# A ring of eight weight tiles, late modulation bound in order, one load per scan system, and gates and attention outputs that stay on chip, in a hybrid attention and DeltaNet block

## The chip, the cores and the metric

The kernel runs on one core of a Trainium2 chip. The metric is the device time of one execution in microseconds; the time before is the median of three runs. The engines are named as in the profile: PE is TensorE (PEld its weight loads), DVE is VectorE, ACT is ScalarE, POOL is GpSimd, and SP is SyncE, which issues most of the DMA transfers. A second queue of DMA issues is ACT's own.

## The reference

One layer over 256 latent tokens and 256 context tokens of width 2048, all in float32. Cut to what matters (heads 8, head width 128, chunk 64):

```python
sh1, sc1, g1, sh2, sc2, g2 = split(silu(c) @ w_ada + b_ada, 6)       # modulation; the context has its own
(lq_a, lkv_a, lk_r, ldq, ldk, ldv, ldz, lda, ldb, lga, lgb) = split_columns(
    modulate(rmsnorm(x, norm_mix), sh1, sc1) @ w_in)                  # and the same for ctx
y_mla = attend_latent(q_l, k_l, v_l, k_c, v_c)       # latent queries over latent and context keys, one softmax

# gated DeltaNet, two directions, chunks of 64: a unit lower triangular system per chunk and head
sol = triangular_solve(m + I, [v * beta, kb * exp(gc)])
v_new = u - w @ s;  s_next = s * g_end + k_end.T @ v_new;  o = (q * exp(gc)) @ s + a @ v_new

y = (sigmoid(lga) * (y_mla @ w_o_mla) + sigmoid(lgb) * (y_dn @ w_o_dn)) @ w_out
x = x + g1 * y
x = x + g2 * conv_glu(modulate(rmsnorm(x, norm_ffn), sh2, sc2), w_ffn_up, ffn_conv, w_ffn_down)
```

The context runs through its own scan first, and its final states start the latent scans. Eight steps of the scan follow each other: four chunks of the context, four of the latent tokens, both directions and all heads side by side.

## The kernel before, in words

**Weights.** Nearly all weights come from DRAM as tiles of 128 x 1024 float32 (512 KB). `raw_w` takes such a tile, named `raw`, from a ring of `NR` buffers (tag "raw", pool `wr`) and issues its load on SP (L127). `split` then makes two parts of it for TensorE: ACT casts the high part `whi` (L121), and DVE subtracts to get the low part `wlo` (L122). TensorE multiplies activations with both. Every matmul is issued through a small wrapper class `Ordered` (L57 to 72) and stands in the profile under its line L68. Where an engine's wrapper is `pinned`, an instruction keeps its place behind the one written before it on that engine; what is not pinned is put in order by a scheduler, from the program's dependences and its own estimates. TensorE is pinned from the attention part on.

**Late modulation.** `ada_rest` computes the part of `w_ada` that is needed late: 128 dots, each one DVE instruction (L279) over a weight tile `rawa` from the same ring (L260) against `sch`. It is a generator that the attention part and the scan advance by a budget (`side`, `fill`), and it loads one tile ahead of its dot.

**Stages, by the time in the profile.** 0 to 56 us: norms, modulation and the first projections (`fp`, `amp`), whose loads are `xl`, `xc`, `wt`, `raw<-in_wadab`, `gr`. Until about 440 us: projections of the DeltaNet inputs (heads, convolution, the key products `U`, `A`). From 440 to 715 us: attention in four passes `b` of two heads each (`mla_project`, `mla_attend`), interleaved with gate projections (`gtp`) and with the inverses of the triangular systems on the side (`inverse`, `off_diagonal`). 715 to 925 us: the DeltaNet scan (`scan`, steps with `kp`, `yp`, `sp`), interleaved with the wd gates' projections and with the attention output's projection (`brp`, weights `womla`). Then the merge, the output projection, and from about 1070 us the ConvGLU.

**Through DRAM.** Results that wait for a later stage lie in DRAM buffers. A triangular system of 64 x 64 is handled as 32 x 32 blocks. `inverse` computes the diagonal blocks in `ux`, a transposed copy is `xt`, and 12 stores on SP (L842) write them to `Xq`; `off_diagonal` computes for q = 0 to 7 the block between them (`uo`) and ACT's queue stores it to `Xo` (L881). In the scan, `load_system` (L1248) collects each step's systems into one of two SBUF tiles `tt` by six DMAs of 32 KB, of which each run in DRAM is 128 bytes; the blocks above the diagonal of a `tt` are zero because POOL cleared the tile once. The gates' `tanh` results `zx` are stored to `Gs` by ACT's queue (L897) and come back as `gt`, four at a time (L1207). Each pass of the attention stores two heads of its output `ryx` to `Ys` (L1140); after the last, the whole of it comes back as `yraw` (1 MB, L1198) and is split into `YM`.

**Queues.** SP and ACT issue their DMAs in program order. Each DMA issue takes one of eight completion semaphores (DMAHW0 to DMAHW7 in the rows below) in turn, for both queues together, and an issue whose semaphore is still held by an earlier DMA waits until that one has landed; the scheduler writes this as a wait.

Of the kernel before, what the change touches and what calls it, by code (L numbers as in the profile page):

```python
# [16 lines left out]
P = 128  # L17
# [12 lines left out]
NR = 5  # L30
# [23 lines left out]
def hybrid_block(ctx: ExitStack, tc: tile.TileContext, io, dbg=None):  # L54
# [45 lines left out]
    dve.memset(ones, 1.0)  # L100
    onesr = const.tile([P, P], F32R, name="onesr")
# [152 lines left out]
    def ada_rest():  # L254
# [9 lines left out]
        half, ahead = None, load(0)  # L264
        for i in range(128):
            c, n = divmod(i, 32)
            h, j = (n // 16 + c) % 2, n % 16
            if h != half:

                for _ in range(1 if i else 0):  # L270
                    yield 1300
                half, sch = h, ad.tile([P, GR], F32, tag="sch", name="sch")
                sync.dma_start(sch, Sc[h])
                for _ in range(3):
                    yield 1300
            w = ahead
            if i < 127:
                ahead = load(i + 1)
            dve.tensor_tensor_reduce(out=w, in0=w, in1=sch, scale=1.0, scalar=0.0, op0=ALU.mult, op1=ALU.add, accum_out=parts[:, h, j : j + 1])  # L279
# [371 lines left out]
    Xq = dram.tile([3, 32, 4, 32, 32], F32, name="Xq")  # L651
    Xo = dram.tile([32, 4, 32, 32], F32, name="Xo")
# [134 lines left out]
    ada.done = 0  # L787
# [30 lines left out]
    def inverse():  # L818
# [20 lines left out]
        for g in range(4):  # L839
            gs = slice(32 * g, 32 * g + 32)  # L840
            for n, x in enumerate((xt, X[:, 0], X[:, 1])):
                sync.dma_start(Xq[n, :, g], x[gs])  # L842
        yield 1000
        pI.close()

    def off_diagonal():
# [7 lines left out]
        def load(q):  # L854
# [4 lines left out]
            for n in range(2):  # L859
                sync.dma_start(xd[:, n], Xq[2 * n, rs].rearrange("r g j c -> (g j) r c"))  # L860
# [4 lines left out]
        for q in range(8):  # L865
# [15 lines left out]
            act.dma_start(Xo[4 * q : 4 * q + 4].rearrange("r g c i -> (g c) r i"), uo)  # L881
# [8 lines left out]
    def gate_fin(ps, out, fin):  # L890
        x = pz.tile([P, T], F32, tag="zx", name="zx")
# [5 lines left out]
        act.dma_start(out, x)  # L897
# [205 lines left out]
    def mla_attend(b):  # L1103
# [29 lines left out]
        def values(h2):  # L1133
# [6 lines left out]
            sync.dma_start(Ys[:, 2 * b + h2], yx)  # L1140
# [30 lines left out]
    tail = iter(())  # L1171
    for b in range(4):
        at, pr = mla_attend(b), mla_project(b + 1) if b < 3 else iter(())
        for n in range(7):
            for st in (pr, tail, at):
                c = next(st, None)
                if c is not None:
                    side(c, R1 if b < 3 else 2.0)
        tail = at
# [5 lines left out]
    gates = gate_tiles([("wgd", f, Gs[1, :, f], None) for f in range(KD)])  # L1185
# [10 lines left out]
    YM = hp.tile([P, HEADS, 2, T], F32R, tag="x16", name="YM")  # L1196
    yraw = pd.tile([P, HEADS, T], F32, tag="o", name="yraw")
    sync.dma_start(yraw, Ys)  # L1198
    split(yraw, YM[:, :, 0], YM[:, :, 1])
# [3 lines left out]
    def branch(w, wh, f, ymat, out):  # L1203

        if f % 4 == 0:
            gt = pd2.tile([P, 4, T], F32, tag="gt", name="gt")
            sync.dma_start(gt, Gs[wh, :, f : f + 4])  # L1207
            gts[wh] = gt
        W = load_w(io[w][f])
# [8 lines left out]
        dve.scalar_tensor_tensor(out=out, in0=gts[wh][:, f % 4], scalar=1.0, in1=ox, op0=ALU.add, op1=ALU.mult)  # L1218
# [5 lines left out]
    def scan():  # L1224
# [5 lines left out]
        for n in range(2):  # L1230
            pool.memset(TTv[n], 0.0)
# [10 lines left out]
        def load_system(n):  # L1242
            st, tt = steps[n], TTv[n % 2]
            for d in range(2):
                for r, c, x in ((0, 0, Xq[1]), (32, 32, Xq[2]), (0, 32, Xo)):
                    rs, cs = slice(64 * d + r, 64 * d + r + 32), slice(c, c + 32)
                    n = 16 * d + 2 * st
                    sync.dma_start(tt[rs, :, cs], x[n : n + 2].rearrange("a g c i -> c (a g) i"))  # L1248
# [122 lines left out]
    fill = Side(e_fill())  # L1371
    pe.pinned = True
# [236 lines left out]
```

## Time and profile before

| | |
|---|---|
| median of 3 runs | 1796.3 us (1796.25 to 1796.43) |
| the profiled execution | 1796.66 us, its span 1794.8 us |
| TensorE busy | 1740.9 us, 97% |
| DVE, ACT, POOL busy | 1353.9, 944.5, 42.1 us |
| DMA | 419.79 MB, 234 GB/s over the span |

The span is what the trace covers, and the execution's own time is 1.9 us longer. Below, a stretch's row gives busy time of each engine, then the clock that TensorE was granted (1.00 is full), the share of time in which the 16 DMA engines were busy (a little over 1 is possible where packets overlap) and the GB/s moved. A row of waits gives total, times and the longest. A row of the timeline gives start, duration, engine, line, operation, and in brackets the idle time before it with what ended it.

### The profile page before, as it was taken

Reading aid. Unit: us, or ns where it says so; the run is one execution under the profiler, and the core shown is the slowest. Engines: PE = TensorE matmul, PEld = TensorE weight load, DVE = VectorE, ACT = ScalarE, POOL = GpSimd, SP = SyncE. Lnnn points to the kernel's source line nnn. Section 1 sums busy time; section 2 is a strip of 40 time slices with the busy share of each in tenths; the row PEclk is TensorE's granted clock in tenths of the full one; section 3 lists DMA queues with packets and bytes.
Section 4 is the critical chain, followed back from the end, with each engine's and each line's share of the span. In section 5 each row is a group of like instructions: output and inputs, shape, how many; then the busy total and the mean of one; then the engine's idle time right before and its main releaser. Section 6 shows DMA issues by size and latency. Waiting matters only on the chain.

```text
span 1794.8 us, 34114 instructions
## 1 busy us (share of the span) xinstructions
PE 1740.9 (97%) x12957; PEld 1504.6 (84%) x12957; DVE 1353.9 (75%) x2692; ACT 944.5 (53%) x1962; POOL 42.1 (2%) x49
## 2 busy tenths in 40 slices
PE   7999999999999999899999989999999999999999
PEld 6787888887888888687878878888888888888888
DVE  4687899879677777576789889887788888755554
ACT  3334544444567666564655546555555555544443
POOL 0000010000000000000010000000000000000000
PEclk9999999999899999999999989999999999999999
DMA  9982788773778767888957966777677777666663
GB/s 383 399 319 89 207 241 241 228 213 104 220 241 260 229 213 249 279 308 309 317 166 240 327 234 224 244 229 229 190 224 226 225 225 225 184 199 199 198 199 122
DMA packets 191493, 419.79 MB, mean 234 GB/s; under 512 B 57248, under 2 KB 97312, under 8 KB 188896
## 3 DMA queue, kind: packets, MB, share of 16 engines
q1 hardware_dynamic: 164144, 402.38, 69.0%
q10 hardware_dynamic: 27184, 15.23, 2.8%
q8 instruction: 102, 1.67, 0.4%
q14 instruction: 63, 0.52, 0.1%
HBM read 388.57 MB, written 28.84 MB: 233 GB/s over the span
## 4 chain that ended last, share of the span: by engine, by line
PE 70%; issue 10%; DMA 9%; DVE 6%; ACT 3%; POOL 1%; SPq 0%; POOLq 0%; DVEq 0%; ACTq 0%
PE fps L68 25%; PE dps L68 13%; PE mmp L68 9%; PE gtp L68 7%; PE fp L68 4%; DMA rawa<-in_wada 4%; DVE wlo L122 2%; PE brp L68 2%; DMA raw<-in_wadab 1%; PE amp L68 1%; DVE rawa L279 1%; DMA raw<-in_wgd 1%; ACT whi L121 1%; PE op L68 1%; DMA raw<-in_wz 1%
## 5 line engine op out<-in xcount | busy, mean ns | idle before, releaser
L122 DVE TENSOR_TENSOR wlo<-raw,whi 128x512 fp32r<-128x512 f32 (+1 forms) x940 | 632.6, 685 | 220.4 <-ACT whi L121 212.1
L121 ACT CAST whi<-raw 128x512 fp32r<-128x512 f32 (+1 forms) x940 | 574.3, 619 | 425.2 <-PE dps L68 113.7
L68 PE MATMUL fps<-H,whi 128*128 128x512 f32 x1376 | 475.1, 394 | 1.7 <-DVE H L1446 1.7
L68 PE MATMUL fps<-H,wlo 128*128 128x256 f32 x1376 | 372.3, 281 | 0.3 <-DVE wlo L122 0.3
L68 PEld LDWEIGHTS fps<-H,whi 128*128 128x128 f32 x1376 | 253.7, 189 | 53.3 <-issue 2.0
L68 PEld LDWEIGHTS fps<-H,wlo 128*128 128x128 f32 x1376 | 259.8, 189 | 7.8 <-DVE wlo L122 0.7
L68 PE MATMUL gtp<-h,whi 128*128 128x512 f32 x640 | 235.1, 404 | 7.4 <-ACT whi L121 7.1
L68 PE MATMUL mmp<-h,whi 128*128 128x512 f32 x640 | 227.1, 397 | 0.0
L68 PE MATMUL dps<-GB,whi 128*128 128x512 f32 (+1 forms) x595 | 195.7, 378 | 0.0
L279 DVE CUSTOM_DVE_ANT_0 rawa<-rawa,sch 128x1024 f32<-128x1024 f32 x128 | 155.8, 1220 | 45.5 <-DMA rawa<-in_wada 41.9
L68 PE MATMUL gtp<-h,wlo 128*128 128x256 f32 x640 | 176.0, 285 | 4.4 <-DVE wlo L122 4.2
L68 PE MATMUL mmp<-h,wlo 128*128 128x256 f32 x640 | 176.0, 281 | 0.6 <-DVE wlo L122 0.6
L68 PE MATMUL dps<-GB,wlo 128*128 128x256 f32 x560 | 154.1, 280 | 0.0
L68 PEld LDWEIGHTS gtp<-h,whi 128*128 128x128 f32 x640 | 121.8, 192 | 34.1 <-ACT whi L121 9.5
L68 PEld LDWEIGHTS mmp<-h,whi 128*128 128x128 f32 x640 | 119.0, 188 | 24.7 <-issue 0.4
L68 PEld LDWEIGHTS gtp<-h,wlo 128*128 128x128 f32 x640 | 122.9, 192 | 11.9 <-DVE wlo L122 7.5
L68 PEld LDWEIGHTS dps<-GB,whi 128*128 128x128 f32 x595 | 109.2, 188 | 21.1
L68 PEld LDWEIGHTS mmp<-h,wlo 128*128 128x128 f32 x640 | 120.3, 188 | 3.9 <-DVE wlo L122 1.3
L68 PEld LDWEIGHTS dps<-GB,wlo 128*128 128x128 f32 x560 | 105.1, 188 | 0.6
L68 PE MATMUL fp<-h,gh 128*128 128x256 f32 (+1 forms) x448 | 85.1, 290 | 2.5 <-ACT h L68 1.7
L68 PEld LDWEIGHTS fp<-h,gh 128*128 128x128 f32 (+1 forms) x448 | 69.4, 189 | 7.6 <-issue 4.1
L517 ACT COPY fx<-fps 128x256 f32<-128x256 f32 x86 | 31.8, 372 | 65.4 <-PE fps L68 65.3
(566 smaller groups left out, 2525.4 us busy)
## 6 DMA issues: line engine op xcount, KB each, us to landing
rawa<-in_wada SPq DMA_DIRECT2D x128, 512.0 KB, 4.7
raw<-in_wgate SPq DMA_DIRECT2D x82, 512.0 KB, 4.3
raw<-in_wval SPq DMA_DIRECT2D x82, 512.0 KB, 4.6
raw<-in_wdown SPq DMA_DIRECT2D x80, 512.0 KB, 4.3
wt<-in_wadas SPq DMA_DIRECT2D x16, 1024.0 KB, 10.8
raw<-in_wadab SPq DMA_DIRECT2D x32, 512.0 KB, 9.2
raw<-in_wgm SPq DMA_DIRECT2D x32, 512.0 KB, 4.7
raw<-in_wgd SPq DMA_DIRECT2D x32, 512.0 KB, 6.1
```

Of the source, the lines that this page charges most:

```text
L68: i = f(*a, **k)
L121: act.copy(hi, raw)
L122: dve.tensor_tensor(out=lo, in0=raw, in1=hi, op=ALU.subtract)
L279: dve.tensor_tensor_reduce(out=w, in0=w, in1=sch, scale=1.0, scalar=0.0, op0=ALU.mult, op1=ALU.add, accum_out=parts[:, h, j : j + 1])
L517: act.copy(out, ps[:M, T:])
```

## The change

- The ring `NR` grows from five tiles to eight. `ada_rest` loads two tiles ahead of its dots, and until the scan begins its dots are issued in order (`odve`), each held behind the DVE instruction written before it; such a dot then shows under the wrapper's line L68.
- A DRAM buffer `Tt` has the layout that the scan reads, zeros included. `inverse` writes the diagonal blocks there by 16 DMAs of 64 KB, `off_diagonal` writes each `uo` by four DMAs of 16 KB on SP, and two DMAs on ACT's queue write the zero blocks from a cleared tile `none`. `load_system` is one DMA of 256 KB. `Xq` keeps only the two parts that `off_diagonal` reads.
- The wd gates from the third on (f = 2 to 15) stay in an SBUF tile `gk`; the other gates go through `Gs` as before.
- `YM` is allocated when the last attention pass begins. Six heads are read back into its low half and split in place, two at a time, during that pass (`heads_back`); the last two heads are split straight from `ryx` and never stored.
- The program reserves 1024 for `dynamic_dma_scratch_size`.

```diff
-NR = 5
+NR = 8
...
+    none = const.tile([P, 32], F32, name="none")
+    pool.memset(none, 0.0)
...
-        half, ahead = None, load(0)
+        half, ahead = None, [load(0), load(1)]
...
-            w = ahead
-            if i < 127:
-                ahead = load(i + 1)
-            dve.tensor_tensor_reduce(out=w, in0=w, in1=sch, ...)
+            w = ahead.pop(0)
+            if i < 126:
+                ahead.append(load(i + 2))
+            (odve if ada.bound else dve).tensor_tensor_reduce(out=w, in0=w, in1=sch, ...)
...
-    Xq = dram.tile([3, 32, 4, 32, 32], F32, name="Xq")
-    Xo = dram.tile([32, 4, 32, 32], F32, name="Xo")
+    Xq = dram.tile([2, 32, 4, 32, 32], F32, name="Xq")
+    Tt = dram.tile([P, 16, 4, 64], F32, name="Tt")
+    for d in range(2):
+        act.dma_start(Tt[64 * d + 32 : 64 * d + 64, :, :, 0:32].rearrange("c s g j -> c (s g) j"), none[:32].unsqueeze(1).broadcast_to([32, 64, 32]))
...
-            for n, x in enumerate((xt, X[:, 0], X[:, 1])):
+            for n, x in enumerate((xt, X[:, 1])):
                 sync.dma_start(Xq[n, :, g], x[gs])
+        for g in range(4):
+            for d in range(2):
+                for b in range(2):
+                    rs = slice(64 * d + 32 * b, 64 * d + 32 * b + 32)
+                    sync.dma_start(Tt[rs, :, g, 32 * b : 32 * b + 32].rearrange("c s j -> s c j"), X[32 * g + 16 * d : 32 * g + 16 * d + 16, b])
...
-            act.dma_start(Xo[4 * q : 4 * q + 4].rearrange("r g c i -> (g c) r i"), uo)
+            for g in range(4):
+                dst = Tt[64 * (q // 4) : 64 * (q // 4) + 32, 4 * (q % 4) : 4 * (q % 4) + 4, g, 32:64]
+                sync.dma_start(dst, uo[32 * g : 32 * g + 32])
...
-        x = pz.tile([P, T], F32, tag="zx", name="zx")
+        kept = isinstance(out, int)
+        x = gk[:, out] if kept else pz.tile([P, T], F32, tag="zx", name="zx")
...
-        act.dma_start(out, x)
+        if not kept:
+            act.dma_start(out, x)
...
-            sync.dma_start(Ys[:, 2 * b + h2], yx)
+            if b < 3:
+                sync.dma_start(Ys[:, 2 * b + h2], yx)
+            else:
+                split(yx, YM[:, 6 + h2, 0], YM[:, 6 + h2, 1])
...
+    def heads_back():
+
+        raw = YM.bitcast(F32)[:, :, 1]
+        sync.dma_start(raw[:, 0:6], Ys[:, 0:6])
+        yield
+        yield
+        for q in range(3):
+            hs = slice(2 * q, 2 * q + 2)
+            split(raw[:, hs], YM[:, hs, 0], YM[:, hs, 1])
+            yield
...
-    gates = gate_tiles([("wgd", f, Gs[1, :, f], None) for f in range(KD)])
+    gates = gate_tiles([("wgd", f, Gs[1, :, f] if f < GD0 else f - GD0, None) for f in range(KD)])
...
-    YM = hp.tile([P, HEADS, 2, T], F32R, tag="x16", name="YM")
-    yraw = pd.tile([P, HEADS, T], F32, tag="o", name="yraw")
-    sync.dma_start(yraw, Ys)
-    split(yraw, YM[:, :, 0], YM[:, :, 1])
+    gk = pd.tile([P, KD - GD0, T], F32, name="gk")
...
-            for d in range(2):
-                for r, c, x in ((0, 0, Xq[1]), (32, 32, Xq[2]), (0, 32, Xo)):
-                    rs, cs = slice(64 * d + r, 64 * d + r + 32), slice(c, c + 32)
-                    n = 16 * d + 2 * st
-                    sync.dma_start(tt[rs, :, cs], x[n : n + 2].rearrange("a g c i -> c (a g) i"))
+            sync.dma_start(tt, Tt[:, 2 * st : 2 * st + 2].rearrange("p a g j -> p (a g) j"))
...
+    ada.bound = False
     pe.pinned = True
```

How instructions move, at the three places of which the prediction speaks. First, the start of ACT's queue; `cv` and `sel` are small inputs, `sq` is the first norm. Before:

```order
L304 DMA cv<-in_cv 128x32
L319 DMA sel<-in_sel 128x3
L307 ACT_TABLE_LOAD
L307 ACTIVATE cth<-cv 128x32
L68 ACTIVATE sq<-xl 128x4x256 x2
L68 COPY scb<-scp 128x512
```

and now:

```order
L306 DMA cv<-in_cv 128x32
L321 DMA sel<-in_sel 128x3
L656 DMA Tt<-none 2048x1x32
L309 ACT_TABLE_LOAD
L309 ACTIVATE cth<-cv 128x32
L68 ACTIVATE sq<-xl 128x4x256 x2
L656 DMA Tt<-none 2048x1x32
L68 COPY scb<-scp 128x512
```

The two zero fills, written far below in the program, were moved to the start of the queue. On SP the semaphores of the first loads shift with them (`xl`, `xc` are the two inputs). Before, the fourth `xc` and the load behind it:

```order
L68 DMA xc<-in_ctxT 128x1024 [waits DMAHW2_49]
L68 DMA wt<-in_wadas 128x2048 [waits DMAHW3_49]
```

and now, where DMAHW4 is the semaphore of the first zero fill:

```order
L68 DMA xc<-in_ctxT 128x1024 [waits DMAHW4_49]
L68 DMA wt<-in_wadas 128x2048 [waits DMAHW5_49]
```

Second, DVE near 520 us, around `km`, which turns the key norms `ks` of TensorE into a scale; `zx` is a gate's value on the way to `Zs`, `s_` and `mns` belong to the softmax. Before:

```order
L518 TENSOR_TENSOR zx<-gtp,zx 128x256
L279 ISA rawa,parts<-rawa,sch 128x1024
L279 ISA parts 128x1
L917 SCALAR_TENSOR_TENSOR zx<-zt,zx 128x256
L122 TENSOR_TENSOR wlo<-raw,whi 128x512
L1118 ISA s__6299,mns<-kbc,sps 128x512
L1118 ISA mns 128x1
L122 TENSOR_TENSOR wlo<-raw,whi 128x512
L1120 TENSOR_SCALAR mns<-mns,qm 128x1
L279 ISA rawa,parts<-rawa,sch 128x1024
L279 ISA parts 128x1
L1022 SCALAR_TENSOR_TENSOR km<-ks,krm 128x4
```

and now:

```order
L520 TENSOR_TENSOR zx<-gtp,zx 128x256
L124 TENSOR_TENSOR wlo<-raw,whi 128x512
L930 SCALAR_TENSOR_TENSOR zx<-zt,zx 128x256
L1131 ISA s__6323,mns<-kbc,sps 128x512
L1131 ISA mns 128x1
L1133 TENSOR_SCALAR mns<-mns,qm 128x1
L124 TENSOR_TENSOR wlo<-raw,whi 128x512
L1035 SCALAR_TENSOR_TENSOR km<-ks,krm 128x4
L1003 CAST rb_h<-km 128x4
L1135 RECIPROCAL mns<-mns 128x1
L68 ISA rawa,parts<-rawa,sch 128x1024
L68 ISA parts 128x1
```

The two dots (`rawa`) that stood between the gate's gather and `km` are gone from there; the next dot stands behind `km`. Third, SP in the scan, from the loads of one step (`jit`: keys and values) to those of the next. Before:

```order
L1253 DMA jit<-KEs 128x1024
L1238 DMA jit<-KTs 128x1024
L1239 DMA jit<-Vs 128x1024
L127 DMA raw<-in_wgd 128x1024
L260 DMA rawa<-in_wada 128x1024
L1248 DMA tt_8861<-Xq 32x8x32 x2
L1248 DMA tt_8861<-Xo 32x8x32
L1248 DMA tt_8861<-Xq 32x8x32 x2
L1248 DMA tt_8861<-Xo 32x8x32
```

and now:

```order
L1278 DMA jit<-KEs 128x1024
L1267 DMA jit<-KTs 128x1024
L1268 DMA jit<-Vs 128x1024
L129 DMA raw<-in_wgd 128x1024
L262 DMA rawa<-in_wada 128x1024
L1273 DMA tt_8909<-Tt 128x512
L129 DMA raw<-in_wgd 128x1024
L129 DMA raw<-in_womla 128x1024
L129 DMA raw<-in_wgd 128x1024 x2
L262 DMA rawa<-in_wada 128x1024 x2
```

Six issues became one; the order of the weight loads around them is as before.

More of the change, by code (lines that the diff above doesn't have):

```diff
@@ L275, in ada_rest @@
                     yield 1300
-            w = ahead
-            if i < 127:
-                ahead = load(i + 1)
-            dve.tensor_tensor_reduce(out=w, in0=w, in1=sch, scale=1.0, scalar=0.0, op0=ALU.mult, op1=ALU.add, accum_out=parts[:, h, j : j + 1])
+            w = ahead.pop(0)
+            if i < 126:
+                ahead.append(load(i + 2))
+            (odve if ada.bound else dve).tensor_tensor_reduce(out=w, in0=w, in1=sch, scale=1.0, scalar=0.0, op0=ALU.mult, op1=ALU.add, accum_out=parts[:, h, j : j + 1])
             if n == 31:
@@ L786, in hybrid_block @@
     ada = Side(ada_rest())
-    ada.done = 0
+    ada.done, ada.bound = 0, True
     ins = {h: head_inputs(h) for h in (3, 0)}
@@ L859, in load @@
             for n in range(2):
-                sync.dma_start(xd[:, n], Xq[2 * n, rs].rearrange("r g j c -> (g j) r c"))
+                sync.dma_start(xd[:, n], Xq[n, rs].rearrange("r g j c -> (g j) r c"))
             return uo, xd
@@ L1171, in hybrid_block @@
     tail = iter(())
+    def heads_back():
[7 more added lines that the diff above has]
+            yield
+    back = iter(())
     for b in range(4):
+        if b == 3:
+            YM = hp.tile([P, HEADS, 2, T], F32R, tag="x16", name="YM")
+            back = heads_back()
         at, pr = mla_attend(b), mla_project(b + 1) if b < 3 else iter(())
@@ L1178, in hybrid_block @@
                     side(c, R1 if b < 3 else 2.0)
+            next(back, None)
         tail = at
@@ L1203, in branch @@
     def branch(w, wh, f, ymat, out):
-        if f % 4 == 0:
+        if f % 4 == 0 and (f == 0 or not wh):
             gt = pd2.tile([P, 4, T], F32, tag="gt", name="gt")
-            sync.dma_start(gt, Gs[wh, :, f : f + 4])
+            n = GD0 if wh else 4
+            sync.dma_start(gt[:, :n], Gs[wh, :, f : f + n])
             gts[wh] = gt
+        gate = gk[:, f - GD0] if wh and f >= GD0 else gts[wh][:, f % 4]
         W = load_w(io[w][f])
@@ L1217, in branch @@
         dve.scalar_tensor_tensor(out=ox, in0=ps[:, :T], scalar=0.5, in1=ox, op0=ALU.mult, op1=ALU.add)
-        dve.scalar_tensor_tensor(out=out, in0=gts[wh][:, f % 4], scalar=1.0, in1=ox, op0=ALU.add, op1=ALU.mult)
+        dve.scalar_tensor_tensor(out=out, in0=gate, scalar=1.0, in1=ox, op0=ALU.add, op1=ALU.mult)
         yield 1300
@@ L1229, in scan @@
         av = ps1.tile([P, HEADS, 64], F32, name="av")
-        for n in range(2):
-            pool.memset(TTv[n], 0.0)
         half_ = [slice(0, 64), slice(64, 128)]
```

2 lines of the change are left out of this document (1 added, 1 removed).

## The prediction

> **What bounds the kernel now.** I read, in this order, the page's busy shares, a table of stretches, TensorE's waits, the DMA queue's waits, the chain of work, and the timeline at the two largest stalls.
>
> ```profile
> PE 1740.9 (97%) x12957; PEld 1504.6 (84%) x12957; DVE 1353.9 (75%) x2692; ACT 944.5 (53%) x1962; POOL 42.1 (2%) x49
> ```
> ```profile
> 20.00:56.00 36.00, 29.77 (x329) 23.06 (x329) 20.25 (x30) 11.13 (x26) 0.81 (x1) 0.91 1.02 418
> ...
> 520.00:530.00 10.00, 8.33 (x72) 7.76 (x73) 7.74 (x21) 5.33 (x14) 2.33 (x2) 0.66 0.77 265
> ...
> 720.00:740.00 20.00, 17.09 (x144) 14.64 (x143) 9.07 (x14) 10.91 (x21) 0.00 (x0) 1.00 0.79 253
> 740.00:760.00 20.00, 15.67 (x129) 12.52 (x129) 12.61 (x28) 11.89 (x31) 0.00 (x0) 1.00 0.84 294
> 760.00:790.00 30.00, 29.40 (x250) 24.81 (x250) 24.05 (x48) 18.43 (x44) 0.00 (x0) 1.00 0.94 332
> ...
> 840.00:860.00 20.00, 18.27 (x216) 15.26 (x215) 12.35 (x27) 10.02 (x21) 0.00 (x0) 0.91 0.86 286
> ...
> 1075.00:1795.00 720.00, 716.29 (x4159) 630.84 (x4158) 519.15 (x965) 376.14 (x711) 0.00 (x0) 1.00 0.67 208
> ```
>
> In the table the first figures are the stretch and its length, then the busy time of TensorE, its weight loads, DVE, ACT and POOL, and last the granted clock, the DMA share and GB/s. TensorE is busy for 1740.9 of 1794.8 us, so at most 54 us of idle time is to be had, plus what the clock loses. The last 720 us hold only 3.7 us of it: nothing that the change does there can pay. What can move is the start, where DMA is the limit (share 1.02), the one stall near 521 us, and the scan from 720 to 860 us.
>
> ```profile
> PE gtp L68 <- ACT whi L121: 7.1, 4, 2.9
> PE gtp L68 <- DVE wlo L122: 4.2, 8, 1.7
> PE ks L68 <- DVE km L1022: 3.7, 1, 3.7
> ```
> ```profile
> SPq L1248 <- DMA Gs<-zx: 23.3, 6, 5.4
> ...
> SPq L127 <- DMA Gs<-zx: 3.9, 1, 3.9
> ...
> SPq L1198 <- DMA Ys<-ryx: 3.5, 1, 3.5
> ```
>
> The first fence is TensorE's waits between 500 and 920 us (total, times, longest), the second those of SP's queue between 700 and 860 us. TensorE waits 7.1 + 4.2 = 11.3 us for split weights of the late gates (gtp). These wait for loads, and the loads wait in SP's queue: seven times, for 23.3 + 3.9 = 27.2 us, SP stood still until a gate store `Gs<-zx` had landed. A small load of the scan cannot need that store's data; the two share one of the eight completion semaphores that the DMA issues go round on, and SP issues in order, so every weight load behind it is late. The chain of work shows one case whole:
>
> ```profile
> 730.82 2.60 DMA Gs<-zx
> ...
> 734.34 5.00 DMA raw<-in_wgd
> ...
> 739.36 0.62 ACT whi L121
> ...
> 740.01 0.70 DVE wlo L122
> ```
>
> **Part 1, the ring and the bound dots.** The eight tiles of the ring let SP issue three loads further ahead, and the late modulation's loads are two ahead instead of one. The stall that this meets:
>
> ```profile
> 516.89 1.22 DVE L279 CUSTOM_DVE_ANT_0 rawa<-rawa,sch 128x1024 f32<-128x1024 f32 x1 [3.20 <-DMA rawa<-in_wada]
> ...
> 518.04 0.42 DVE L917 SCALAR_TENSOR_TENSOR zx<-zt,zx 128x256 f32<-128x256 f32 x1
> ```
> ```profile
> 518.50 0.51 ACT L918 ACTIVATE zx<-zx,onh 128x256 f32<-128x256 f32 x1 [2.88 <-DVE zx L917]
> ...
> 521.02 0.60 ACT L1011 ACTIVATE ksq<-kps 128x512 f32<-128x512 f32 x1
> ```
> ```profile
> 521.67 0.60 PE L68 MATMUL ks<-ones,ksq 128*32 128x1 f32 x32 [3.75 <-DVE km L1022]
> ```
>
> DVE sat 3.20 us in front of a dot whose weights were late; zx (L917) stood behind it, ACT's L918 behind that, ksq behind ACT's copies, and TensorE's ks behind ksq for 3.75 us. In the new order no dot stands between the gather of zx and km, and the dots' loads have a longer lead. Without the 3.20 us the gap is 3.75 - 3.20 = 0.55 us. The clock of 0.66 over 520 to 530 means 2 x (1 - 0.66) x 10 = 6.8 us at half rate, from about 520.5 to 527.3; TensorE worked from 521.67, so 5.6 us at half cost 2.8 us. At most 3.2 + 2.8 = 6.0 us come back, at least 0 (another instruction can be late there, as ACT's next exponential now stands ahead of ksq). I take 5.
>
> The Trainium skill, "TensorE: Matmul & The Clock Gate", section "What's actually happening", says that half rate follows at least one idle window of about 3.4 us, and that one busy window of 3413 ns restores full rate. By that rule the 0.55-us gap leaves no half rate, and the site gives the full 6.0, so the sum would be 1 us lower. The trace agrees here (a 3.75-us gap, then 6.8 us at half), but the clock of 0.91 at 840 to 860 stands beside idle time of only 20 - 18.27 = 1.73 us; so I don't lean on it.
>
> The price of the binding: a dot now may not slip behind ready work on DVE.
>
> ```profile
> DVE rawa L279 <- DMA rawa<-in_wada: 41.9, 35, 4.2
> ```
> ```profile
> SPq L260 <- DVE parts L279: 27.0, 13, 4.5
> ```
>
> Of 41.9 us in 35 waits over the kernel, the one of 3.2 us above is the only one behind an entry of TensorE's list above. Longer lead shortens such waits; a second tile held by a dot lengthens SP's waits for dots (27.0 us in 13). A wait of the mean size, 41.9/35 = 1.2 us, reaching TensorE once where none did before is the new cost that I book: +1.5 with part 2's waits below. Bounds: -1.2 (one more such wait vanishes) to +4.2 (the longest dot wait reaches TensorE).
>
> **Part 2, systems through one layout in DRAM.**
>
> ```profile
> ux<-Ud SPq DMA_DIRECT2D x1, 1024.0 KB, 7.1
> ...
> tt<-Xq SPq DMA_DIRECT2D x32, 32.0 KB, 5.7
> ...
> tt<-Xo SPq DMA_DIRECT2D x16, 32.0 KB, 4.0
> ```
>
> These are the DMA issues: count, size, median time to landing. Per system six DMAs of 32 KB (256 runs of 128 bytes each) become one of 256 KB. That frees five semaphore turns and five issues per step, 40 in all, from the place in SP's queue where the 23.3 us were lost. The writes grow: 16 `Tt<-ux` of 64 KB replace 4 writes on SP near 446 us, and four `Tt<-uo` on SP replace each of eight stores on ACT's queue.
>
> ```profile
> 456.60 0.93 SPq L860 DMA_DIRECT2D xd<-Xq  x2
> 466.10 0.35 SPq L127 DMA_DIRECT2D raw<-in_wz  x1
> ```
>
> Two issues took 0.93 us, so net 12 more take 12 x 0.47 = 5.6 us of SP at the first place. Right behind it SP issued nothing from 457.5 to 466.1, 8.6 us, which takes the 5.6: so 0. For the 32 others SP now waits for ACT's copy uo, with weight loads behind it. A Gs wait was 23.3/6 = 3.9 us; eight such would be 31 us of SP, and in the scan 27.2 us of SP waits made 11.3 of TensorE's: so +13 at worst, but these loads now run ahead on eight tiles, and a uo wait of a microsecond is hidden. It is in the +1.5. The two memsets on POOL (off the path) are worth 0.
>
> The zero blocks of the layout are new: two DMAs of 2048 runs of 128 bytes, which the order puts third and eighth on ACT's queue, in the stage that DMA bounds.
>
> ```profile
> 3.54 10.23 DMA xc<-in_ctxT
> 13.80 12.48 DMA raw<-in_wadab
> ```
> ```profile
> q1 hardware_dynamic: 164144, 402.38, 69.0%
> q10 hardware_dynamic: 27184, 15.23, 2.8%
> ```
>
> The chain of the first 30 us goes through these two loads, so DMA time added there is added to the end. Price of 4096 small packets: queue q1 has 2451 bytes and 0.69 x 16 x 1794.8 / 164144 = 121 ns per packet, q10 560 bytes and 29.6 ns. By bytes alone (512 KB at 418 GB/s) it is 1.25 us; at q10's mean 4096 x 29.6 / 16 = 7.6 us; on the straight line through both (2.5 ns + 0.0483 ns per byte, 8.7 ns at 128 bytes) 2.2 us. Then SP: its fourth `xc` load now waits on the semaphore that the first zero block uses, so the queue runs dry until that lands; the shortest landing of any tt DMA, nearest in form, was 1.6 us. I take 2.2 + 1.6 = +3.8; the ends are +1.25 and 7.6 + 2 x 1.6 = +10.8.
>
> ```profile
> DMA to landing us min/median/max: 1.6/5.4/9.8
> ```
>
> The Trainium skill, "DMA: Bandwidth & Descriptors", section "Specifications", states that below 512 bytes a DMA engine does a read-modify-write. It gives no time, so the sum stands; by that rule the upper end is the likelier one. The trace agrees in direction: 32 KB in short runs took 5.7 us to land.
>
> **Parts 3 and 4, gates on chip, attention output.** 14 of 32 stores `Gs<-zx` and 3.5 of 8 reloads `gt<-Gs` go. All the waits behind such stores in the scan are of this kind, since the wd gates run through it, and only two wgd gates still store. The 1 MB reload with its one split is replaced by six heads read before the scan and split in three pieces:
>
> ```profile
> L121 ACT CAST YM<-yraw x1: 1906/1906/1906, 725.8 to 725.8; 128x2048 fp32r<-128x2048 f32 x1
> L122 DVE TENSOR_TENSOR YM<-yraw,YM x1: 2293/2293/2293, 727.7 to 727.7; 128x2048 fp32r<-128x2048 f32 x1
> ```
>
> The same 1.9 us of ACT and 2.3 of DVE move to before 715 us in four portions, and SP's 3.5-us wait for Ys moves with them, ahead of the gates' loads: 0, hidden by the ring. If that cover fails, the first gtp is 3.5 us late.
>
> With parts 1 to 3 the 11.3 us of gtp waits lose their cause. The stretches above show 2.91 us idle at 720 to 740 and 4.33 at 740 to 760. I take four fifths, 9.0 us, since some loads stay late behind bursts of jit loads, and 1 of the 1.8 us that clock 0.91 cost at 840 to 860: -10.0. Bounds 0 and 13.1.
>
> **Sum.** The profiled execution took 1796.66 us, 0.36 above the median. Against it: +3.8 - 5 - 10.0 + 1.5 = -9.7; on the median, 1786.6.
>
> **Rivals.** (A) *The zero fill costs its upper end*, 10.8 instead of 3.8: 1793.6, no change. For it: short runs are slow in every row; against: 512 KB is little beside 1.25 MB per 3 us there. It decides if the start (first fp) moves by over 7 us. (B) *Supply stays the bound of the scan*: the DMA share is 0.94 at 760 to 790, so the wgd loads may be late whatever SP does; then the 10 us don't come, 1796.6, no change. Against: it is only 0.79 to 0.84 where the gaps are. (C) *Slower: the scan's own operands come late in place of the weights.*
>
> ```profile
> 737.70 0.43 SPq L1238 DMA_DIRECT2D jit<-KTs  x1
> ```
> ```profile
> 747.75 1.90 PE kp L68 x32
> ```
> ```profile
> jit<-KTs SPq DMA_DIRECT2D x8, 512.0 KB, 7.1
> ```
>
> kp (L68) reads jit in each step; issued at 737.7, it lands after 7.1 us in the median, 3.0 us before kp. A ring of eight may put up to three more weight loads, 3 x 1.25 = 3.75 us, ahead of it; jit is then 0.75 us late at the median and 3.75 at a landing 3 us above it. At 2.5 us in each of seven steps that is +17.5, while the gtp waits (-11.3) are covered by it: 1796.3 + 3.8 - 5 + 6.2 + 1.5 = 1802.8. It decides once jit lands more than about 1.6 us after kp could start. Against: the order keeps nearly the same count of loads between two steps, and no kp wait is in TensorE's list. (D) *All comes back*: 1796.3 + 2.2 - 6.0 - 13.1 = 1779.4.
>
> **Chances.** Forecast 0.52 (own range 1781 to 1792.5), A 0.13, B 0.13, C 0.10, D 0.12. A measurement of this kernel tells about 0.2% (3.6 us) from no change. Faster: forecast and D 0.64, and 0.07 from the lower half of A, 0.01 of B: 0.72. Same: 0.06 of A and 0.08 of B, 0.14. Slower: C and 0.04 of B, 0.14. The range leaves out the far half of D and most of C: 1778 to 1799.
>
> **What the profile after would show.** First fp 2 to 6 us later, with SP waiting on `Tt<-none`; the ks gap near 521 below 1 us and clock 1.0 there; no SP wait on `Gs<-zx` above 1 us at L1273; gtp waits below 3 us; kp not in the list. I am wrong if dots wait more than 41.9 us in all, if kp waits, or if the start moves by 8 us.

## The result, and the profile after

The changed kernel took 1786.61 us in the median of six runs, the kernel before 1796.75 us in six runs beside it; the ratio is 0.9941 with a 95% interval of 0.9927 to 0.9954. One of the six runs before took 1906.24 us, far above the other five (1796.25 to 1797.47), and is not in the ratio. A second comparison gave 0.9945 (0.9923 to 0.9966). So it is faster by 0.6%. The forecast 1786.6 was met, but not by its terms: three of them were off by 3.6 to 7.8 us, in opposite directions. The profiled execution took 1786.89 us, its span 1785.1.

The stretches of the changed kernel, in the columns of the prediction's table:

```profile
20.00:56.00 36.00, 30.65 (x328) 23.96 (x332) 17.50 (x25) 11.13 (x24) 1.02 (x1) 0.81 1.02 414
...
460.00:510.00 50.00, 41.30 (x299) 36.56 (x298) 29.84 (x60) 24.90 (x58) 2.01 (x2) 0.86 0.73 198
510.00:520.00 10.00, 10.00 (x101) 8.66 (x101) 7.99 (x17) 7.84 (x20) 1.18 (x1) 1.00 0.86 300
520.00:530.00 10.00, 10.00 (x57) 8.54 (x55) 5.69 (x15) 6.12 (x14) 0.00 (x0) 1.00 0.78 229
...
720.00:740.00 20.00, 20.00 (x120) 17.28 (x123) 12.48 (x22) 9.26 (x19) 0.00 (x0) 0.91 1.00 381
740.00:760.00 20.00, 20.00 (x203) 17.07 (x192) 15.71 (x34) 15.16 (x39) 0.00 (x0) 1.00 1.00 371
760.00:790.00 30.00, 30.00 (x260) 25.93 (x257) 25.25 (x50) 18.33 (x44) 0.00 (x0) 1.00 0.94 349
...
840.00:860.00 20.00, 20.00 (x272) 17.56 (x271) 14.63 (x30) 13.37 (x34) 0.00 (x0) 1.00 0.97 357
```

TensorE has no idle time at all from 720 to 860 us; but 8.7 us of the 50 from 460 to 510 are idle, at a clock of 0.86, where the kernel before was busy for 47.8. Since TensorE's order is nearly the same in both kernels, its matmuls can be paired, and the time at which the same matmul starts gives a running account (one profile of each kernel; a second profile of the changed kernel, further below, differs from this one by up to 4.1 us):

| place | before, us | after, us | after less before | step |
|---|---|---|---|---|
| second projection in the start (fp) | 53.58 | 57.61 | +4.0 | +4.0 |
| convolution's prefix sums (eps) | 154.19 | 161.16 | +7.0 | +2.9 |
| split of kvn, before the stall (gtp) | 455.14 | 461.50 | +6.4 | -0.6 |
| after the key norms of pass 0 (gtp) | 471.06 | 485.24 | +14.2 | +7.8 |
| after the key norms of pass 1 (gtp) | 526.20 | 534.75 | +8.6 | -5.6 |
| last pass (ptp) | 699.82 | 704.52 | +4.7 | -3.9 |
| after the last yps (gtp) | 715.66 | 723.94 | +8.3 | +3.6 |
| the scan's gates end (gtp) | 850.98 | 842.31 | -8.7 | -17.0 |
| end of the last projection (dps) | 1778.94 | 1769.28 | -9.7 | -1.0 |

Three losses that the runs below bear on stand in it. (The +2.9 at the prefix sums is not one of them: it is missing in the second profile of the changed kernel.) The first is the start. The fences show SP's queue, ACT's queue, SP's wait over the whole kernel, and TensorE:

```profile
5.57 0.33 SPq L68 DMA_DIRECT2D xl<-in_xT  x1
15.58 0.33 SPq L68 DMA_DIRECT2D xc<-in_ctxT  x1
```
```profile
1.67 0.67 ACTq L656 DMA_DIRECT2D Tt<-none  x1
```
```profile
SPq L68 <- DMA Tt<-none: 9.7, 1, 9.7
```
```profile
36.21 0.53 PE L68 MATMUL fp<-h,gh 128*96 128x256 f32 x1 [0.56 <-DVE h L68]
```

The fourth `xc` was issued at 15.6 instead of 5.7 us, because the first zero fill held its semaphore until it landed, and the fp that started at 30.64 starts at 36.21. Of these 5.6 us the later loads gave 1.5 back by 57 us.

The second loss is new. SP's queue, DVE and TensorE near 480 us, and SP's wait there:

```profile
460.33 17.87 SPq L851 DMA_DIRECT2D Tt<-ux  x16
478.24 2.53 SPq L869 DMA_DIRECT2D xd<-Xq  x4
```
```profile
480.60 0.16 DVE L1035 SCALAR_TENSOR_TENSOR km<-ks,krm 128x4 f32<-128x4 f32 x1 [10.91 <-DMA xd<-Xq]
```
```profile
480.91 0.60 PE L68 MATMUL ks<-ones,ksq 128*32 128x1 f32 x32 [6.51 <-DVE km L1035]
```
```profile
SPq L851 <- DMA Zs<-zx: 6.6, 2, 6.2
```

The small tile km takes over memory that the inverse's tile `ux` held; in the order of the program it waits for DMAs on all eight semaphores, that is for every store out of `ux`. (The view names `xd<-Xq`, which uses the same semaphores right behind; the program has km wait for the stores.) Before the change the 12 stores were through at about 455.8 us, some 10 us before km. Now SP issues 24; the ninth `Tt<-ux` stood 6.2 us behind a gate store `Zs<-zx`, which ACT issued only at 470.27 us, and the last landed at about 480. DVE stood for 10.9 us, TensorE for 6.5, and the low clock did the rest.

The third loss is the wait for the last attention product, 3.52 us against 1.87. The chain of work there shows two late-modulation dots (`rawa`) on DVE in front of the last split of PT:

```profile
713.38 1.12 DVE rawa L281
...
717.92 1.13 DVE rawa L68
```
```profile
719.72 1.45 PE L68 MATMUL yps<-PT,V 128*128 128x512 f32 x7 [3.52 <-DVE PT L124]
```

The gain of the scan shows in SP's list for 700 to 860 us, where the waits for gate stores stood at the top:

```profile
SPq L1267 <- PE kp L68: 21.3, 5, 6.9
SPq L129 <- DVE wlo L124: 16.2, 16, 3.8
SPq L1273 <- PE yp L68: 9.4, 5, 2.3
```

SP now waits for TensorE to release the scan's operands: the loads run ahead of their use.

### The profile page after: what moved, and what is told of

It is laid out like the page before. It is cut to its first block, busy times and chain, and to the rows that moved or that the text cites. A ratio compares the mean times of both kernels' runs of the same rounds, so it can differ in the third digit from the quotient of the medians.

```text
span 1785.1 us, 34155 instructions
## 1 busy us (share of the span) xinstructions
PE 1737.5 (97%) x12957; PEld 1507.2 (84%) x12957; DVE 1356.8 (76%) x2696; ACT 950.5 (53%) x1966; POOL 41.4 (2%) x48
## 4 chain that ended last, share of the span: by engine, by line
PE 63%; issue 8%; DMA 1%; DVE 1%; ACT 0%; SPq 0%; POOL 0%; POOLq 0%; DVEq 0%
PE fps L68 27%; PE dps L68 13%; PE gtp L68 11%; PE brp L68 3%; PE vps L68 1%; PE kps L68 1%; PE qps L68 1%; PE sps L68 1%; PE kp L68 1%; PE ivp L68 1%; PE op L68 1%; PE yps L68 1%; PE yp L68 0%; DMA YM<-Ys 0%; SPq L851 0%
## 5 line engine op out<-in xcount | busy, mean ns | idle before, releaser
L68 PE MATMUL fps<-H,whi 128*128 128x512 f32 x1376 | 475.0, 394 | 3.1 <-DVE H L1472 3.1
L68 PE MATMUL fps<-H,wlo 128*128 128x256 f32 x1376 | 372.3, 280 | 0.0
L68 PEld LDWEIGHTS fps<-H,whi 128*128 128x128 f32 x1376 | 253.7, 189 | 54.7 <-issue 1.9
L68 PEld LDWEIGHTS fps<-H,wlo 128*128 128x128 f32 x1376 | 259.7, 189 | 7.5 <-DVE wlo L124 0.5
L68 PE MATMUL gtp<-h,whi 128*128 128x512 f32 x640 | 231.4, 399 | 0.0
L68 PE MATMUL mmp<-h,whi 128*128 128x512 f32 x640 | 229.5, 400 | 0.0
L68 PE MATMUL dps<-GB,whi 128*128 128x512 f32 (+1 forms) x595 | 195.7, 377 | 0.0
L68 PE MATMUL mmp<-h,wlo 128*128 128x256 f32 x640 | 177.5, 283 | 0.0
L68 PE MATMUL gtp<-h,wlo 128*128 128x256 f32 x640 | 173.9, 282 | 0.0
L68 PE MATMUL dps<-GB,wlo 128*128 128x256 f32 x560 | 155.2, 282 | 0.0
L68 PEld LDWEIGHTS gtp<-h,whi 128*128 128x128 f32 x640 | 120.5, 190 | 25.3 <-issue 0.9
L68 PEld LDWEIGHTS mmp<-h,whi 128*128 128x128 f32 x640 | 119.8, 189 | 24.9 <-ACT dkx L531 0.3
L68 PEld LDWEIGHTS dps<-GB,whi 128*128 128x128 f32 x595 | 109.2, 188 | 20.2
L68 PEld LDWEIGHTS gtp<-h,wlo 128*128 128x128 f32 x640 | 121.5, 190 | 4.5
L68 PEld LDWEIGHTS mmp<-h,wlo 128*128 128x128 f32 x640 | 121.8, 190 | 3.6 <-issue 1.4
L68 PEld LDWEIGHTS dps<-GB,wlo 128*128 128x128 f32 x560 | 105.8, 189 | 0.6
L68 PE MATMUL fp<-h,gh 128*128 128x256 f32 (+1 forms) x448 | 85.5, 291 | 2.5 <-ACT h L68 1.7
L68 PEld LDWEIGHTS fp<-h,gh 128*128 128x128 f32 (+1 forms) x448 | 69.7, 190 | 7.6 <-issue 4.1
L68 DVE CUSTOM_DVE_ANT_0 rawa<-rawa,sch 128x1024 f32<-128x1024 f32 x60 | 72.9, 1218 | 0.0
```

Source lines behind the costliest of these rows:

```text
L68: i = f(*a, **k)
```

## The experiments

In the following, time is the median with the ratio to the kernel before on the same chip; single runs of the kernel before spread from 1789 to 1803 us on those chips, so that stalls are read from the profiles and the ratios' intervals decide on totals.

**Zero fills late.**

```diff
-        act.dma_start(Tt[64 * d + 32 : ...], none...)      # written with the DRAM buffers
+            oact.dma_start(Tt[64 * d + 32 : ...], none...)  # in inverse(), behind the load of ux, in order
```

> The changed kernel with the two zero fills held back in ACT's order to the time of the inverses (near 390 us), nothing else moved. Theory (the fills at the start block SP's fourth context load for 9.7 us): first fp back from 36.2 to 30.6 us within 0.5, SP's wait on the fills gone, and the end 4 to 5.5 us earlier, near 1782. Rival (the later loads of the start absorb the delay, as two microseconds of it were absorbed by 57 us): at most 1.5 us earlier. Second rival (the fills cost the same at their new place): no gain at the end, and a stall near 390 us.

1789.07 us, ratio 0.9962 (0.9945 to 0.9979). The start came back nearly as expected: the matmul that stood at 27.9 us came 5.9 us earlier, the first fp stands at 31.3 us (30.6 within 0.5 was expected), and all of it was lost again before 405 us. The chain of work, and TensorE:

```profile
391.11 7.13 DMA ux<-Ud
```
```profile
400.76 1.22 PE L68 MATMUL bc_ps<-ident,ms 128*128 128x128 f32 x4 [5.37 <-POOL ms L175]
```

The fills were issued on ACT's queue at 379 and 384 us, and SP's load of ux went out 5.6 us behind the store of QEs instead of 2.8. DVE waited 13.8 us for it, and the norm that TensorE needed was behind it on DVE: `ms` starts at 399.7 us, after the first step on ux at 398.3. In the changed kernel the norm stands ahead of that step (397.6 and 402.8), and TensorE waits 0.7 us there. So the second rival held in its effect, no gain at the end and a stall near 390 us. The order on DVE changed together with the fills' place, and how much of the stall belongs to each is not separated.

**The systems' path as before.**

```diff
-            sync.dma_start(tt, Tt[:, 2 * st : 2 * st + 2]...)
+            for d in range(2):
+                for r, c, x in ((0, 0, Xq[1]), (32, 32, Xq[2]), (0, 32, Xo)):
+                    sync.dma_start(tt[rs, :, cs], x[n : n + 2]...)     # and Xq, Xo written as before, no fills
```

> The changed kernel with the systems' path as before the change (Xq with three parts, Xo on ACT's queue, six loads of 32 KB per step, no zero fills); ring of eight, bound dots, gates on chip and early heads stay. Theory: first fp at 30.6; the 6.5-us ks stall near 481 falls below 1 us with its half clock, since only the twelve old stores hold the memory that km takes over; so 4 + 7.8 us come back, and the scan loses little, under 4 us, because with no gate store on ACT's queue the six small loads wait only for loads: 1775 to 1779. Rival (one load per system is what freed the scan): waits for weights (gtp) of 6 us and more come back between 720 and 860 us, and the end is 1780 or later.

1779.3 us, ratio 0.9913 (0.9883 to 0.9943). Both sides of the new layout are in it. By 721 us this kernel was 16.7 us ahead of the changed one: 5.9 at the start, 7.6 at the ks stall, which fell to the 2.19 us of before, 2.0 in the low clock behind it, and the rest in small steps. From 722 to 860 us it lost 10.3 of them, against either profile of the changed kernel. TensorE's waits between 500 and 920 us:

```profile
PE gtp L68 <- DVE wlo L122: 3.3, 7, 1.7
PE gtp L68 <- ACT whi L121: 2.0, 2, 1.7
```

So one load per system is worth about 10 us of the scan's 17, and its stores and fills cost some 17 before the scan. The theory had the first part too small.

**All gates through DRAM.**

```diff
-    gates = gate_tiles([("wgd", f, Gs[1, :, f] if f < GD0 else f - GD0, None) for f in range(KD)])
+    gates = gate_tiles([("wgd", f, Gs[1, :, f], None) for f in range(KD)])
```

> The changed kernel with all wd gates stored to DRAM and reloaded as before; all else stays. Theory (the gate stores' semaphores held SP up in the scan): SP's waits on Gs stores return with several microseconds each, gtp waits of 3 to 8 us return between 720 and 860 us, the end 4 to 9 us later than the changed kernel, 1790 to 1796. Rival (eight tiles cover these waits): gtp waits stay under 1 us and the end moves by less than 1.5 us.

1786.77 us, ratio 0.9948 (0.9932 to 0.9964); the profile ends 1.1 us later than the changed kernel's, and from 722 to 900 us the account between the two moves by only 0.05 us. SP's waits came back, TensorE's did not:

```profile
SPq L129 <- DMA Gs<-zx: 11.7, 3, 5.8
...
SPq L262 <- DMA Gs<-zx: 4.2, 1, 4.2
```

15.9 us of such waits cost nothing with eight tiles and one load per system: the rival held. Part 3 of the change is worth nothing that can be told here. What the gate stores cost in the kernel before, with five tiles and six loads, was not tried by itself.

**Ring of five.**

```diff
-NR = 8
+NR = 5
```

> The changed kernel with a ring of five weight tiles; two late-modulation loads ahead, all else stays. Theory: with the gate stores gone SP rarely stands still, so the scan keeps most of its gain; gtp waits of 1 to 4 us between 720 and 860 us, the end 1 to 5 us later, 1788 to 1791. Rival (the ring's depth is what covers the scan): gtp waits of 8 us or more, 1795 or later. In both, two rawa tiles of five held before 715 us may show a new weight wait there.

1855.94 us, ratio 1.0328 (1.0292 to 1.0365): 70 us slower than the changed kernel. The account against it grows from 160 us on in many steps of one to eight microseconds, the largest at gate projections, and stands at 59 us by 691 us; only 4.8 us fall between 722 and 900 us. TensorE's list over the kernel begins with

```profile
PE gtp L68 <- ACT whi L123: 23.6, 7, 8.0
```

Both theories were wrong about the place: the deep ring pays in the attention part, more than in the scan. My reading is that with two loads ahead two of five tiles belong to dots, and three are too few for the weights. That is read from the program: no run tried the changed kernel with five tiles and one load ahead.

**The ring alone, on the kernel before.**

```diff
-NR = 5
+NR = 8
```

> The kernel before the change with the ring of eight tiles alone (and the freed scratch that makes room for it); one modulation load ahead, dots unbound. Theory: the ring lets weights run past SP's stops; of the 11.3 us of gtp waits between 720 and 860 us 5 to 9 us go, the 521 stall stays since its dot has still one load of lead: 1786 to 1792. Rival (the six small loads per step take the semaphores and hold SP whatever the ring): gtp waits stay above 8 us, end within 3 us of before.

1793.05 us, ratio 0.9983 (0.9963 to 1.0003): no change that can be told; its profiled execution, the slowest of its ten, is 5 us longer. In the scan the waits fell from 11.3 to 7.0 us, though SP stood behind gate stores for 34.1 us in nine waits, five of them at the scan's small loads:

```profile
PE gtp L68 <- ACT whi L121: 4.3, 3, 1.7
...
PE gtp L68 <- DVE wlo L122: 2.7, 7, 1.2
```
```profile
SPq L1248 <- DMA Gs<-zx: 15.5, 5, 4.6
```

The stall of 3.75 us at ks fell to 0.82 and 1.76 us (ks and the vps behind it), but a late `qps` of 3.4 us took its place near 615. DVE's wait for a dot's weights did not go:

```profile
521.38 0.42 DVE L917 SCALAR_TENSOR_TENSOR zx<-zt,zx 128x256 f32<-128x256 f32 x1
...
526.57 1.22 DVE L279 CUSTOM_DVE_ANT_0 rawa<-rawa,sch 128x1024 f32<-128x1024 f32 x1 [3.56 <-DMA rawa<-in_wada]
```

DVE stood for 3.56 us in front of a dot here too. In this kernel's order the dot stands behind the gate's zx, so that ksq no longer waits for it, and only km does.

**Dots unbound.**

```diff
-    ada.done, ada.bound = 0, True
+    ada.done, ada.bound = 0, False
```

> The changed kernel with the late modulation's dots left to the scheduler from the beginning (two loads ahead, ring of eight, all else stays). Theory (the stall of 3.75 us at 521 us before the change came from a dot put ahead of the gate's chain while its load was late; two loads ahead cure it, the binding is neutral): no ks stall above 1 us near 530, end within 2 us of the changed kernel's 1786.6. Rival (the binding is what removed it): DVE stands again 2 to 4 us in front of a dot with a TensorE gap of 2 us or more between 500 and 700 us, end 3 to 8 us later.

1797.76 us, ratio 1.0012 (0.9991 to 1.0032): 10 us slower than the changed kernel in the profiles (spans of 1795.4 and 1785.1), the whole gain. DVE's waits for dots' weights over the kernel, in this kernel and in the changed one:

```profile
DVE rawa L281 <- DMA rawa<-in_wada: 51.4, 47, 5.5
```
```profile
DVE rawa L281 <- DMA rawa<-in_wada: 19.4, 23, 1.7
```

I read this so: left free, the scheduler draws a dot ahead of the work written before it, as soon as its own estimate has the weights there, and DVE stands in front of it. The binding is a brake. No single gap is the 10 us: 2.5 are lost by 485 us, 1.7 more by 654, 2.6 by 693, and 3.5 by the end of the scan. Pieces of this size also lie between two profiles of one kernel; the total is clear of that, its places are not. The site at 530 us stays free of a ks stall, so there the binding is not needed, as the theory said; its end was wrong.

**Attention output as before.**

```diff
-                split(yx, YM[:, 6 + h2, 0], YM[:, 6 + h2, 1])
+            sync.dma_start(Ys[:, 2 * b + h2], yx)      # all heads; yraw, one load and one split
```

> The changed kernel with the attention output as before: all eight heads stored, one reload of 1 MB and one split after the last pass. Theory (the early splits of the six heads lengthen the chain to the last PT on ACT and DVE, 3.5 us of yps wait against 1.9 before the change): yps wait back to 1.5 to 2.2 us, and the 4.2 us of splitting is hidden behind gate projections; end 0 to 3 us earlier. Rival (early heads free SP of the wait for Ys and let the gates' weights run ahead): gtp waits of 2 us or more between 720 and 760 us, end 1 to 4 us later.

1782.86 us, ratio 0.9919 (0.989 to 0.9948), which overlaps the changed kernel's intervals; the profile ends 1.3 us earlier, and is 1.9 us ahead at 161 us already, where the second profile of the changed kernel is 1.8 us ahead too. The wait for the last attention product:

```profile
PE yps L68 <- DVE PT L124: 3.1, 1, 3.1
```

It is nearly as long without the early heads, and no gtp wait appeared: neither theory held. Part 4 is worth nothing that can be told, either way.

**Fill in the middle of the off-diagonal work, eight stores.**

```diff
+                sync.dma_start(Tt[32 * b : 32 * b + 32, :, g, ...].rearrange("c n j -> n c j"), X[32 * g : 32 * g + 32, b])  # 8 stores
+            if q == 4:
+                osync.dma_start(Tt[32:64, :, :, 0:32]..., none...)       # one fill, on SP
```

> The changed kernel with the diagonal blocks stored by 8 DMAs of 128 KB instead of 16 of 64 KB (the layout in DRAM puts both directions' chunks in one index, and a system is read by two loads of 128 KB), and the zeros written by one DMA on SP in the middle of the off-diagonal work, near 600 us. Theory (the price of the new layout is where its stores stand, not their bytes): first fp at 30.6, no new stall near 390 us, ks stall near 480 smaller than 6.5 us because SP passes 16 stores instead of 24 before the xd loads (1 to 4 us if one store still shares a semaphore with a late Zs store), scan without gtp waits: 1773 to 1779. Rival (the fills cost the same wherever they stand, as they did near 390 us): a stall of 3 us or more near 600 us, and the end above 1782.

1781.59 us, ratio 0.9911 (0.9884 to 0.9939). With 16 stores instead of 24 the ks stall is gone (only the 2.19 us before it stay), and at 485 us this kernel is 15.3 us ahead of the changed one. Then 10 us are lost at one place. SP's queue, ACT and TensorE:

```profile
568.88 1.27 SPq L865 DMA_DIRECT2D xd<-Xq  x2
578.10 2.62 SPq L888 DMA_DIRECT2D Tt<-uo  x4
580.76 0.43 SPq L129 DMA_DIRECT2D raw<-in_wkvb  x1
```
```profile
584.92 1.14 ACT L123 CAST whi<-raw 128x512 fp32r<-128x512 f32 x2 [3.92 <-DMA raw<-in_wkvb]
```
```profile
585.59 0.58 PE L68 MATMUL vps<-whi,kvn 128*128 128x256 f32 x1 [7.45 <-ACT whi L123]
```

With the fill there, the scheduler put the four stores of the next uo ahead of the load of wkvb in SP's queue (with the fill near 420 us, below, they stand behind it). ACT could not have that uo before TensorE reached its matmuls, at their fixed place; SP stood 8 us for it, the weights of wkvb behind, and DMA was busy for only 0.18 of 570 to 580 us. That is the head-of-line wait that the prediction named for these stores. So the rival's stall came, but from the order of SP's queue: the fill had landed at 570.4 us, before most of that wait.

**Fill near 420 us.**

```diff
+            if j == 18:     # in inverse()
+                dve.tensor_scalar(out=none[:32], in0=flat[:32, 0:32], scalar1=0.0, scalar2=None, op0=ALU.mult)
+                sync.dma_start(Tt[32:64, :, :, 0:32]..., none...)        # and the eight stores
```

> The changed kernel with the diagonal blocks stored by 8 DMAs of 128 KB, a system read by two loads, and the zeros cleared on DVE out of the inverse's own tile and written by one DMA on SP when the inverse is two thirds done (near 420 us, where DMA is quiet and no store of U or load of ux stands behind it). Theory (the price of the layout is what stands behind its writes in SP's queue): first fp at 30.6, no stall near 390, ks stall near 480 below 1 us, no stall near 585, since no fill delays uo there; scan without gtp waits: 1768 to 1773 in the profile. Rival (stores of uo on SP, with weight loads behind them, cost some microseconds by themselves between 500 and 700 us): a wait of SP for uo above 3 us with a weight wait of TensorE behind it, 1774 to 1780.

1774.11 us, ratio 0.9871 (0.9853 to 0.989): the best of all, 13 us under the changed kernel on the same chip. The longest waits of TensorE from 150 to 920 us, and a stretch of the scan:

```profile
PE yps L68 <- DVE PT L123: 3.5, 1, 3.5
PE kps L68 <- ACT kvn L122: 2.4, 1, 2.4
PE ks L68 <- ACT ksq L1022: 2.2, 1, 2.2
```
```profile
740.00:760.00 20.00, 20.00 (x176) 17.15 (x172) 18.07 (x39) 14.56 (x36) 0.00 (x0) 1.00 1.03 375
```

The scan keeps all of its gain, and the two losses at the start and near 480 us are gone (16.2 us ahead at 484). What stands behind the writes was the price, as the theory said. For km this can be seen in SP's waits:

```profile
SPq L867 <- DMA Zs<-zx: 7.2, 1, 7.2
```

SP stood behind a late gate store here as well (and for 4.9 us in the run before), but with eight stores fewer this came at the load of xd, behind the last store out of ux. So km did not wait.

**Stores of uo on ACT's queue.**

```diff
-                sync.dma_start(dst, uo[32 * g : 32 * g + 32])
+                act.dma_start(dst, uo[32 * g : 32 * g + 32])
```

> As the kernel with the fill near 420 us, and the four stores of each uo on ACT's queue instead of SP's. By the theory it equals that kernel within 1.5 us, since the waits for uo cost nothing once no fill delays them; by the rival it is 3 us or more faster, with no wait of SP for uo. A third way: 28 issues of some 0.4 us more on ACT delay the splits' high parts, and it is 1 to 4 us slower.

1778.98 us, ratio 0.9905 (0.9885 to 0.9924): slower than with the stores on SP, by 2.4 us in the profiles and 4.9 in the medians; the intervals touch. SP's wait for uo left, another came:

```profile
SPq L864 <- DMA Tt<-uo: 16.6, 8, 4.8
```

The next reload of uo waits until the stores out of that tile have landed. A stall of 0.86 us at `rps` near 496 us and small ones up to 576 make up the loss: the size is the third way's, the mechanism none of the three.

**The changed kernel again.**

> The changed kernel itself, on the same chip as the two others, to compare with them and with the kernel before: 1784 to 1789, ratio to before 0.993 to 0.996, and in its profile the same stalls as in the first one (ks near 481 us of 5 us or more, first fp near 36 us), since these hang on the order of SP's queue and not on chance.

1787.42 us, ratio 0.9945 (0.9923 to 0.9966). The ks stall was 7.7 us, SP's wait for the fill 9.5: the same places. Its account against the first profile of the same kernel shows how far two single profiles differ: it is 1.8 us ahead at 161 us, 1.2 behind at 500, 4.0 behind at 721 and 4.1 at the end. Over 155 to 165 us, where the first has the +2.9, its granted clock is 1.00 against 0.83. So a piece of 4 us or less, in the table or in an experiment, is a single reading; the ks stall, the scan and the first fp stand in both profiles.

**No dot before the last PT.**

```diff
-        ada(AD * c)
+        if not last:            # set when the last pass begins
+            ada(AD * c)
...
-    ada.bound = False
```

> The kernel with the fill near 420 us and the uo stores on SP, with no late-modulation dot advanced during the last attention pass, and the dots bound through the scan too, so that none is pulled up from there. Theory (the 3.5-us yps stall just before the scan is two dots of 1.2 us on DVE ahead of the last PT split): yps wait 1 to 1.5 us, 2 us and a half-clock window of 3.4 us less there; if the scan takes the dots without loss, 1769 to 1773, else up to 1778. Rival (the wait comes from the splits of weights and of the six heads, as it was there before the change with 1.9 us): yps wait stays above 3 us.

1775.9 us, ratio 0.9892 (0.9872 to 0.9913), against 0.9871 without these two edits: no gain. The wait fell from 3.5 to 2.1 us, so the dots were 1.4 us of it and the rest is other work:

```profile
PE yps L68 <- DVE PT L123: 2.1, 1, 2.1
```

At 890 us this kernel was 5.2 us ahead of that one; then the dots that it had put off stood in front of the norm behind the output projection:

```profile
1043.04 0.39 PE L68 MATMUL ss<-ones,x1q 128*32 128x1 f32 x16 [4.31 <-ACT x1q L1447]
1046.44 1.22 PE L68 MATMUL b<-ident,ms 128*128 128x128 f32 x4 [3.01 <-POOL ms L174]
```

The theory held for the site in direction, at two thirds of its size, and the time was given back later. That the dots cause these later waits is read from the edit and the place; it was not tried by itself.

## Why the prediction was right, and where it was not

- **Start, +3.8.** It cost 5.6 at the first fp and 4.0 by 57 us. Both terms were mis-sized. The hold of SP's fourth `xc` behind the fill's semaphore lasted 9.7 us, not the 1.6 that I booked: the fill took 13.9 us from issue to landing. It cost less than it lasted, because the loads already issued kept DMA busy meanwhile (share 0.90 from 0 to 20 us, as before). But in this time 267 GB/s were moved instead of 339. The packet records of the trace show why: the fills' 4096 packets of 128 bytes took 13.1 ns each on average, which is 4096 x 13.1 / 16 = 3.4 us of all engines, where the straight line gave 8.7 ns and 2.2 us. By this estimate most of the 4.0 is the packets and little of it the hold; no run has one without the other. Rival A's price was not reached.
- **The stall at 521, -5.** TensorE was busy without a gap from 510 to 530 us at full clock, and the account shows -5.6: right in place and size. With the ring alone some 3 us of it come, by an order in which the late dot stands behind the gate's zx, and not by earlier weights.
- **The scan, -10.** It was -17.0: all 11.97 us of idle time and the slow clock came back, and the upper bound of 13.1 was passed. Idle time and clock make 13.7; some 3 us more are not idle time in the records and stay open. The cause that I put first, the gate stores' semaphores, is not what the change was paid for: with those waits back, nothing was lost. The six small loads per step are 10 us of it. The ring alone took 4.3 us off the waits there, and the gates on chip nothing that can be told.
- **Stores of the diagonal blocks, 0.** This is the step that failed most: "Right behind it SP issued nothing from 457.5 to 466.1, 8.6 us, which takes the 5.6: so 0". SP's idle time was no cover, because the stores also hold memory that DVE needs next, and one of them shared a semaphore with a store not yet issued. It cost 7.8 us. The order showed it: km waits there for DMAs on six semaphores before, and on eight now, and I hadn't read that row. Where the wait behind the late gate store fell behind the last store out of ux, in the runs with eight stores fewer, this cost was gone.
- **The binding, +1.5.** The sign was wrong. I priced a dot that may not slip back; by the run without it, what binding does is to keep a dot from being drawn forward, and the kernel is 10 us slower when it is left out.
- **Attention output, 0.** Right within what can be told. The yps wait before the scan grew by 1.7 us and its slow clock, which no step of mine had; at most 1.4 of the wait is dots.

- **In no term.** The -3.9 between 526 and 700 us: 2.2 of it is idle time of TensorE from 530 to 700 us that the changed kernel does not have, and the kernel with unbound dots loses 3.9 over the same stretch again, which points to the binding. It is a single reading.

So an upper bound missed in the scan and a gain priced as a cost made up for two losses that were not booked, the stores and the wait before the scan. That the total met the forecast to the microsecond is luck; what was right is the way it moved, and the three places at the start, at 521 us and in the scan. The signs that the prediction named for the profile after came, but none of them looked at 480 us.

The rule of the Trainium skill, "TensorE: Matmul & The Clock Gate", section "What's actually happening", is about 3.4 us idle, then half rate in windows of that length. Two places here agree with it. Behind the 3.52-us gap the clock of 0.91 over 720 to 740 us is 2 x 0.09 x 20 = 3.6 us at half. Around the 6.51-us gap 0.86 over 50 us is 14 us, four such windows. Other places do not: the clock of 0.83 over 155 to 165 us, 3.4 us at half, stands behind a gap of only 1.53 us, and before the change gaps of 2.94 and 2.14 us, ending at 740.0 and 753.4 us, left the clock at 1.00 over 740 to 760. So the length of one gap does not decide it here.

## What to carry to other kernels

Its bytes alone do not give a transfer's price: ask how short its packets are, what stands behind it in the issuing queue, who holds the completion semaphore that it will take, and which tile takes over its source's memory, for that tile waits until the store has landed. Idle time of a queue covers an issue only if no engine waits for the transfer itself. When parts of a change are judged by their total, pair the matmuls of the two traces and read the account by place, with a second profile of the same kernel beside it to see how far chance goes; here a 10-us gain was 28 us of gains less 18 of losses, and moving the fill and halving the sixteen stores gave 13 us more.

## What the runs showed of the hardware

- Two fills of 2048 runs of 128 bytes took 13.9 and 7.3 us to land while loads of 512 KB were queued (in the start), 6.6 us for 4096 runs near 565 us, where the DMA share was 0.61 from 560 to 570.
- Packets of 128 bytes took 13.1 ns each in the fills of the start and 13.6 ns in the fill near 430 us: 3.4 to 3.5 us of the 16 engines for 4096 of them.
- From 700 to 860 us, SP's waits on gate stores of 15.9 us, with eight tiles and one load per system, went with no wait of TensorE for weights. 34.1 us of them with eight tiles and six loads went with 7.0 us, and 27.2 us with five tiles and six loads with 11.3.
